# Seven half-block products for the up projections of a two-layer decoder step on one Trainium2 core

## The chip, the cores and the metric

The kernel runs on one core of one Trainium2 chip, as a single launch. A core has five engines with instruction queues of their own: PE (TensorE, matrix products into PSUM), DVE (VectorE), ACT (ScalarE), POOL (GpSimd) and SP (SyncE, which here only issues DMAs). Each works through its queue in order and waits on semaphores. The metric is the device time of one execution in microseconds (us). Before the change three runs took 1202.59, 1202.91 and 1203.35 us; the median, 1202.91, is the number to compare with.

## The reference

One inference step of a two-layer decoder trunk. 512 prompt rows and 8 x 4 sample rows, 544 in all, go through both layers: a token mixer (causal pooling in layer 0, a gated linear recurrence, HGRN2, in layer 1), then a gated feed-forward block with a causal convolution of width 3. The feed-forward block is what the change is about:

```python
D_MODEL, D_FF, CONV_W = 1024, 2816, 3

def conv_ffn(h, ctx, w_up, conv_w, conv_b, w_down):
    L = h.shape[1]
    u = h @ w_up                                  # (rows, 1024) @ (1024, 2 * 2816)
    full = jnp.concatenate([ctx.astype(u.dtype), u], axis=1)
    c = conv_b + sum(full[:, j:j + L] * conv_w[j] for j in range(CONV_W))
    gate, val = jnp.split(c, 2, axis=-1)
    y = (jax.nn.gelu(gate, approximate=True) * val) @ w_down
    return y, full[:, -(CONV_W - 1):]
```

Around every sub-layer stand RMS norms: `h = rmsnorm(x, norm_ffn_pre)`, and afterwards `x = x + rmsnorm(m, norm_ffn_post)`. All data are float32; the outputs are the rows after both layers and the new states.

## The kernel before

**Layout.** Features lie on the 128 partitions, the 544 rows (TOK) along the free axis, so x is 8 tiles (KT) of 128 x 544. A product is built from weight blocks of 128 output features; a block of an up projection has 8 k-tiles of 128 x 128.

**Precision.** Each float32 operand is split in two fp32r parts, high and low. `mm3` issues three matmuls for each k-tile and half of the rows: high by high, high by low, low by high. ACT makes the high part of a weight (`wh<-raw`), DVE the low part (`wl<-raw,wh`), 512 columns (four k-tiles) at a time. For some blocks (`DW`, `by_dma`) both parts come by DMA from POOL's queue instead: one plain load, a negated copy on ACT, one adding load.

**Feed-forward block** (`ffn`). The 2816 hidden features are 22 pairs of blocks (NPAIR), a gate block j and a value block 22 + j. PARTS = (8, 7, 7) cuts them into three parts. In each part all up blocks run first (`block`: 8 k-tiles x 2 halves x 3 matmuls, of 256 and 288 columns, into two PSUM banks of a tile `ps`); then the eight down products run over the pairs of that part, and DVE adds the second and third part to the sum `m`. The first six blocks go through `group`, which begins while the norm of the second half of the rows is still in work. After each up block:

- DVE multiplies the PSUM result by the row scale R of the norm (`evac_full`, into `t`),
- ACT and DVE make the convolution (`conv`: one ACT step, two DVE steps of 560 columns),
- after the value block, DVE multiplies it with the gelu of the gate, and ACT and DVE split the result for the down products (`finish`).

POOL copies the convolution's context in and out (`fst`) and, in the first part, issues the weight loads of `DW`.

**Order.** All of it is recorded by `Plan` and put in order at build time by a list scheduler (`emit`) with its own table of costs, latencies, and slots of the buffer pools; what comes out is a fixed order for each engine. Weights are one stream; `ensure(i + LOOK)` has the splits of the next three blocks recorded ahead. Raw weight tiles (`raw`, 128 x 1024) have 3 buffers, the split tiles (`wh`, `wl`) 10 each, the working tiles `t` 22, PSUM 2 double banks (`ps`) and 4 single ones (`pa`).

Of the kernel before, what the change touches and what calls it, by code (L numbers as in the profile page):

```python
# [36 lines left out]
PARTS = (8, 7, 7)  # L37
# [12 lines left out]
DW = ((2, 6), (3, 9), (3, 9))  # L50
# [289 lines left out]
def trunk_step(ctx: ExitStack, tc: _tile.TileContext, xT, xp, xs, spool, s0, fctx, par, gb0, cst, bands,  # L340
# [29 lines left out]
    up_i, dn_i = {}, {}  # L370

    def add_ffn(li):
        p0 = 0
        for pi, n in enumerate(PARTS):
            for j in range(p0, p0 + n):
                up_i[li, j] = len(stream)
                stream.append((wup[li, j], KT))
                up_i[li, NPAIR + j] = len(stream)
                stream.append((wup[li, NPAIR + j], KT))
            for o in range(KT):  # L380
                dn_i[li, pi, o] = len(stream)
                stream.append((wdn[pi][li, o], n))
            p0 += n
# [16 lines left out]
    bases = (0, min(hin_i.values()), min(up_i[1, j] for j in range(2 * NPAIR)))  # L400
# [5 lines left out]
    special = {}  # L406
    nxt = [0]

    def ensure(upto):
        while nxt[0] <= min(upto, len(stream) - 1):  # L410
            i = nxt[0]
            nxt[0] += 1
            src, kc = stream[i]
            if not by_dma(i):
                raw = tt((P, 512)) if kc * P <= 512 else wp.tile([P, KT * P], F32, tag="raw", name="raw")
                SP.dma_start(raw[:, 0:kc * P], src)
            chunks = []
            for c0 in range(0, kc, 4):
                n = min(4, kc - c0) * P
                if i in special:  # L420
                    sp, q = special[i]
                    wh, wl = sp[q + len(chunks)], sp[q + 2 + len(chunks)]
                else:
                    wh = wp.tile([P, 4 * P], F32R, tag="wh", name="wh", bufs=10)
                    wl = wp.tile([P, 4 * P], F32R, tag="wl", name="wl", bufs=10)
                if by_dma(i):

                    h, l, w = wh[:, 0:n], wl[:, 0:n], src[:, c0 * P:c0 * P + n]
                    POOL.dma_start(h, w)
                    ACT.activation(l, h.bitcast(F32), AF.Identity, scale=-1.0)  # L430
                    POOL.dma_start(l, w, accum_op=ALU.add)
                    chunks.append((wh, wl))
                    continue
                r = raw[:, c0 * P:c0 * P + n]
                ACT.activation(wh[:, 0:n], r, AF.Identity)
                DVE.tensor_tensor(wl[:, 0:n], r, wh[:, 0:n].bitcast(F32), op=ALU.subtract)
                chunks.append((wh, wl))
            prepared[i] = chunks
# [107 lines left out]
    x = one.tile([P, KT, TOK], F32, name="x")  # L546
# [117 lines left out]
    class Residual:  # L664
# [10 lines left out]
        def start_b(self, hf):  # L675
# [13 lines left out]
            def low(k):  # L689
                DVE.scalar_tensor_tensor(getx(ol)(k, sl), x[:, k, sl], pcol(gnext + k), oh[:, k, sl].bitcast(F32),  # L690
                                         op0=ALU.mult, op1=ALU.subtract)

# [133 lines left out]
    for hf, c in ((0, 0), (0, 4), (1, 0), (1, 4)):  # L826
        SP.dma_start(x[:, c:c + 4, HV[hf]], xT[:, c:c + 4, HV[hf]])
# [20 lines left out]
    def ffn(li, XH, XL, res, enter, mtile, leave, n_ahead, hv=HV):  # L848

        R = res.rnext  # L850
        cst_t = rp.tile([P, 17 * ROUND_A], F32, tag="fst", name="fst", bufs=1)[:, 0:2 * NPAIR * 18]
# [66 lines left out]
        def do_down(pi, o, src, sl):  # L918
            if o == 0 and pi == 2 and acc[0] is None:
                acc[0] = tt()  # L920
# [8 lines left out]
            if pi < 2:  # L929
# [10 lines left out]
        p0 = 0  # L940
        for pi, n in enumerate(PARTS):
            if pi == 1 and li == 0:
                plan.after(m0[:, KT - 1, :])
# [4 lines left out]
            j0 = p0  # L948
            blocks = []
            for j in range(p0, p0 + n):  # L950
                blocks += [j, NPAIR + j]
            if pi == 0:
                first, blocks = blocks[:GRP_U], blocks[GRP_U:]
                ensure(up_i[li, first[-1]])
                us_ = {}

                def each(g, o, hf):
                    if hf == 0:
                        us_[g] = new_u(first[g])
                    evac_half(*us_[g], o, hf)  # L960
                    if hf == 1:
                        finish(*us_[g], first[g])
                        ensure(up_i[li, first[g]] + GRP_U)
                group([up_i[li, j] for j in first], rH, rL, KT, each, enter(res), (4, 2),
                      (4, 2), (0, 1, 2, 3))
            for j in blocks:
                i = up_i[li, j]
                ensure(i + LOOK)
                t = block(i, rH, rL, KT, HP)
                u, us = new_u(j)  # L970
                evac_full(u, us, t)
                finish(u, us, j)
            yH = lambda k, sl: ys[j0 + k][0][:, sl]
            yL = lambda k, sl: ys[j0 + k][1][:, sl]

            i0, i1 = dn_i[li, pi, 0], dn_i[li, pi, 1]
            ensure(i1 + LOOK - 1)
            t0, t1 = ps2(), ps2()
            for ks in (range(n - 1), range(n - 1, n)):
                for t, i in ((t0, i0), (t1, i1)):  # L980
                    for k in ks:
                        for hf in range(2):
                            mm3(t[:, hf, 0:HT], i, k, yH, yL, slice(hf * HT, (hf + 1) * HT), k == 0, k == n - 1)
# [569 lines left out]
```

## Time and profile before

| | |
|---|---|
| median of three runs | 1202.91 us |
| the profiled execution | 1202.7 us, of which 1200.9 from first to last instruction |
| pooling mixer until the first up product of layer 0 | 0 to 42.8 us |
| feed-forward block, layer 0: up products of the three parts start at | 42.8, 196.1 and 322.1 us |
| its down products start at | 147.5, 279.8 and 405.8 us |
| HGRN2 mixer of layer 1 | 452.4 us, its output products from 726.9 us |
| down products of layer 1 start at | 878.6, 1011.9 and 1138.8 us |
| moved by DMA | 120.39 MB, 100 GB/s in the mean |

A row of the view of groups reads: line, engine, operation, written tile<-read tiles, shapes, count | busy us, mean ns of one | idle time before, and what ended it. L306 is the line of the scheduler that issues nearly everything, so groups are told apart by tile names: `wh`, `wl` weights, `raw` their float32 form, `ps` and `pa` PSUM, `t` working tiles, `xh`, `xl`, `oh`, `k` the split rows, `m` the sum of the down products. A row of the timeline reads: start us, length us, engine, the same names, count [idle before]. A row of a window reads: from:to, length, then busy us (x instructions) of PE, its weight loads, DVE, ACT and POOL, the granted clock of PE, and the DMA share.

### The profile page before, as it was taken

Reading aid. Unit: us, or ns where it says so; the run is one execution under the profiler, and the core shown is the slowest. Engines: PE = TensorE matmul, PEld = TensorE weight load, DVE = VectorE, ACT = ScalarE, POOL = GpSimd, SP = SyncE. Lnnn points to the kernel's source line nnn. Section 1 sums busy time; section 2 is a strip of 40 time slices with the busy share of each in tenths; the row PEclk is TensorE's granted clock in tenths of the full one; section 3 lists DMA queues with packets and bytes.
Section 4 is the critical chain, followed back from the end, with each engine's and each line's share of the span. In section 5 each row is a group of like instructions: output and inputs, shape, how many; then the busy total and the mean of one; then the engine's idle time right before and its main releaser. Section 6 shows DMA issues by size and latency. Waiting matters only on the chain.

```text
span 1200.9 us, 25513 instructions
## 1 busy us (share of the span) xinstructions
PE 1180.8 (98%) x10268; PEld 1147.4 (96%) x10268; DVE 777.6 (65%) x1809; ACT 561.2 (47%) x1139; POOL 215.7 (18%) x513
## 2 busy tenths in 40 slices
PE   8999999999999999999999999999999999999996
PEld 7899999999999997999999999999999999999995
DVE  6787733765367666688878985468742666457635
ACT  4655434443244455556555554546432444234441
POOL 3431101110011132111121131324100111011113
PEclk9999999999999999999999999999999999999998
DMA  9732222223222355423322223436222222322202
GB/s 320 169 91 71 89 88 88 88 78 99 88 89 97 106 142 127 107 87 104 109 94 83 90 91 120 124 63 149 86 82 86 84 83 75 106 88 84 78 30 75
DMA packets 43223, 120.39 MB, mean 100 GB/s; under 512 B 5339, under 2 KB 9819, under 8 KB 43097
## 3 DMA queue, kind: packets, MB, share of 16 engines
q1 hardware_dynamic: 30336, 91.71, 23.6%
q0 software_dynamic: 12624, 27.01, 9.5%
q8 instruction: 81, 1.33, 0.5%
q14 instruction: 38, 0.30, 0.1%
q10 hardware_dynamic: 144, 0.05, 0.0%
HBM read 110.79 MB, written 8.31 MB: 99 GB/s over the span
## 4 chain that ended last, share of the span: by engine, by line
PE 93%; DMA 3%; DVE 2%; ACT 1%; issue 0%; SPq 0%; DVEq 0%; ACTq 0%
PE ps L306 74%; PE pa L306 17%; PE pr L306 2%; DMA raw<-wup 1%; DMA k<-xp 1%; DVE t L306 1%; DVE m L306 1%; DMA k<-wup 0%; ACT t L306 0%; ACT wh L306 0%; PE pa L1449 0%; SPq L306 0%; DVE o L306 0%; ACT m L306 0%; DVE x L306 0%
## 5 line engine op out<-in xcount | busy, mean ns | idle before, releaser
L306 ACT ACTIVATE wh<-raw 128x512 fp32r<-128x512 f32 (+1 forms) x312 | 193.0, 620 | 336.9 <-PE ps L306 319.4
L306 PE MATMUL ps<-xh,wh 128*128 128x256 f32 (+1 forms) x1072 | 313.3, 292 | 0.0
L306 PE MATMUL ps<-xl,wh 128*128 128x256 f32 (+1 forms) x1072 | 309.8, 289 | 0.0
L306 PE MATMUL ps<-xh,wl 128*128 128x256 f32 (+1 forms) x1072 | 307.8, 287 | 0.0
L306 DVE TENSOR_TENSOR wl<-raw,wh 128x512 fp32r<-128x512 f32 (+1 forms) x312 | 210.0, 675 | 141.1 <-ACT wh L306 132.6
L306 PE MATMUL ps<-t,wh 128*128 128x272 f32 x1184 | 223.6, 288 | 0.8 <-ACT m L306 0.7
L306 PEld LDWEIGHTS ps<-xh,wl 128*128 128x128 f32 x1072 | 202.0, 188 | 2.8 <-issue 2.6
L306 PEld LDWEIGHTS ps<-xh,wh 128*128 128x128 f32 x1072 | 202.0, 188 | 2.5 <-issue 0.2
L306 PEld LDWEIGHTS ps<-xl,wh 128*128 128x128 f32 x1072 | 201.7, 188 | 2.6 <-issue 1.6
L306 PE MATMUL ps<-oh,wl 128*128 128x256 f32 (+2 forms) x688 | 198.4, 288 | 0.0
L306 PE MATMUL ps<-k,wh 128*128 128x256 f32 (+2 forms) x688 | 198.1, 288 | 0.0
L306 PE MATMUL ps<-oh,wh 128*128 128x256 f32 (+2 forms) x688 | 198.0, 288 | 0.0
L306 PEld LDWEIGHTS ps<-t,wh 128*128 128x128 f32 x1184 | 185.6, 188 | 1.7 <-ACT m L306 1.1
L306 DVE TENSOR_TENSOR t<-t 128x512 f32<-128x512 f32 (+10 forms) x332 | 141.3, 450 | 52.1 <-ACT t L306 46.4
L306 PE MATMUL ps<-t,wl 128*128 128x272 f32 x592 | 170.4, 288 | 0.0
L306 DVE SCALAR_TENSOR_TENSOR t<-t,prm 128x560 f32<-128x560 f32 (+1 forms) x184 | 146.8, 801 | 36.1 <-ACT t L306 33.1
L306 POOL COPY fst<-t 128x16 f32<-128x16 f32 (+1 forms) x176 | 73.0, 450 | 439.8 <-DVE t L306 439.5
L306 DVE TENSOR_TENSOR t<-ps,R 128x512 f32<-128x512 f32 (+1 forms) x216 | 86.3, 433 | 76.0 <-PE ps L306 74.4
L306 ACT ACTIVATE t<-t 128x544 fp32r<-128x544 f32 (+5 forms) x145 | 85.5, 600 | 98.8 <-DVE t L306 95.7
L306 PEld LDWEIGHTS ps<-k,wh 128*128 128x128 f32 x688 | 129.7, 189 | 0.5 <-issue 0.5
L306 PEld LDWEIGHTS ps<-oh,wh 128*128 128x128 f32 x688 | 129.8, 189 | 0.0
L306 PEld LDWEIGHTS ps<-oh,wl 128*128 128x128 f32 x688 | 129.2, 188 | 0.0
(174 smaller groups left out, 1645.3 us busy)
## 6 DMA issues: line engine op xcount, KB each, us to landing
raw<-wup SPq DMA_DIRECT2D x78, 512.0 KB, 3.3
raw<-wdn SPq DMA_DIRECT2D x32, 448.0 KB, 3.3
raw<-win SPq DMA_DIRECT2D x26, 512.0 KB, 3.3
raw<-wdn SPq DMA_DIRECT2D x16, 512.0 KB, 3.2
wh<-wup POOLq DMA_DIRECT2D x16, 256.0 KB, 3.6
wl<-wup POOLq DMA_DIRECT2D x16, 256.0 KB, 5.7
t<-s POOLq DMA_DIRECT2D x16, 256.0 KB, 4.0
o_hs<-t POOLq DMA_DIRECT2D x16, 256.0 KB, 2.4
```

The costliest lines, as they stand in the source:

```text
L306: o[1](*o[3], **o[4])
```

## The change

The pairs 6 to 21 of each layer (16 of 22) are computed with seven products of half blocks. A and B are the two weight blocks of a pair, each cut in two along k (512 columns each); the rows are cut in two halves of 272 (U). For each pair:

- **Weights.** `seventh` forms seven 512-column operands: four are halves of A and B as loaded, three are sums, made by four additions on POOL. All seven are split in high and low on ACT and DVE, in place of four splits before. Both raw tiles stay until the last split.
- **Rows.** `operands`, once a layer during part 0, forms the sums and differences of the row halves from x, its gain and R (so R no longer comes in afterwards); DVE scales, POOL adds, ACT and DVE split (`both`). They take the place of x and of the tiles xh and xl; x is therefore saved to yT and loaded again after the last such pair.
- **Products.** `seven` runs 7 x 4 x 3 matmuls of 272 columns into three `pa` banks, some started and some added to, with a step on ACT or DVE after each product to combine them.

Down products now have five parts, PARTS = (6, 4, 4, 3, 5); those of a part are spread between the pairs of the next one by MIX; weights are recorded nine units of four k-tiles ahead. DVE adds four parts to `m` instead of two. More blocks have their weights made by DMA: entries 2 to 11 instead of 2 to 5 of layer 0, 3 to 11 instead of 3 to 8 of layer 1.

```diff
-PARTS = (8, 7, 7)
+PARTS = (6, 4, 4, 3, 5)
+MIX = ((4, 4, 0, 0), (3, 3, 2, 0), (3, 3, 2), (2, 2, 2, 2, 0))
+SEVEN = PARTS[0]
-DW = ((2, 6), (3, 9), (3, 9))
+DW = ((2, 12), (3, 9), (3, 12))
...
+    def seventh(i, q):
+        H = 4 * P
+        if q == 0:
+            raws[i] = A_, B_ = [wp.tile([P, KT * P], F32, tag="raw", name="raw") for _ in range(2)]
+            for t, src in zip((A_, B_), stream[i][0]):
+                SP.dma_start(t, src)
+            mine[i] = dict(sums) or {q: tt((P, H)) for q in range(2)}
+            POOL.tensor_tensor(mine[i][0], A_[:, 0:H], B_[:, 0:H], op=ALU.add)
+            POOL.tensor_tensor(B_[:, 0:H], B_[:, 0:H], B_[:, H:2 * H], op=ALU.add)
+            POOL.tensor_tensor(mine[i][1], B_[:, 0:H], A_[:, 0:H], op=ALU.add)
+        A_, B_ = raws[i]
+        if q == 6:
+            POOL.tensor_tensor(A_[:, H:2 * H], A_[:, H:2 * H], mine[i][1], op=ALU.add)
+        return (mine[i][1], A_[:, 0:H], mine[i][0], B_[:, 0:H], A_[:, H:2 * H], B_[:, H:2 * H], A_[:, H:2 * H])[q]
...
+        def operands(k, out):
+            za, hold = tt(), out["hold"]
+            zb, w, s_ = hold[:, k], hold[:, 6 + k % 2], hold[:, 4 + k // 2, U[k % 2]]
+            for z, f in ((za, k), (zb, k + 4)):
+                DVE.scalar_tensor_tensor(z, x_of(f), pcol(gn + f), R, op0=ALU.mult, op1=ALU.mult)
+                SP.dma_start(yT[:, f], x_of(f))
+            POOL.tensor_tensor(w[:, U[0]], za[:, U[1]], zb[:, U[1]], op=ALU.subtract)
+            POOL.tensor_tensor(w[:, U[1]], za[:, U[0]], za[:, U[1]], op=ALU.subtract)
+            POOL.tensor_tensor(za[:, U[1]], za[:, U[0]], w[:, U[0]], op=ALU.subtract)
+            POOL.tensor_tensor(s_, zb[:, U[0]], za[:, U[1]], op=ALU.subtract)
+            both(out["a", k], za)
...
+            Y, X, Z = banks
+            c, t = w[:, U[0]], w[:, U[1]]
+            after = (lambda: ACT.activation(c, Y, AF.Identity),
+                     lambda: DVE.tensor_tensor(t, c, X, op=ALU.subtract),
+                     lambda: DVE.tensor_tensor(c, t, Z, op=ALU.add),
+                     lambda: second(1, ALU.subtract, c, Y),
+                     lambda: ACT.activation(u_of(0)[0][:, 2:2 + HT], X, AF.Identity),
+                     lambda: DVE.tensor_tensor(u_of(1)[0][:, 2:2 + HT], c, Z, op=ALU.add),
+                     lambda: second(0, ALU.subtract, Y, t))
+            for q, (o, more) in enumerate(((Y, 0), (X, 0), (Z, 0), (Y, 0), (X, 1), (Z, 0), (Y, 1))):
+                ahead_units(unit0[i] + q)
+                wh, wl = prepared[i][q]
+                for k in range(4):
+                    xh_, xl_ = operand(q, k)
+                    sl = slice(k * P, (k + 1) * P)
+                    for e, (a, b) in enumerate(((wh, xh_), (wh, xl_), (wl, xh_))):
+                        PE.matmul(o, a[:, sl], b, start=(not more and k == 0 and e == 0), stop=(k == 3 and e == 2),
+                                  skip_group_check=True)
+                after[q]()
...
+        sums.clear()
+        for q in range(4):
+            xt[q] = big.tile([P, 2, TOK], F32, tag=f"X{q}", name="x")
+            SP.dma_start(xt[q], yT[:, 2 * q:2 * q + 2])
```

How this moves instructions is seen in the order on three engines. First DVE, near the end of the first part of layer 0 before the change: one pair of blocks (evacuations from `ps_374` and `ps_382`), with the weight splits of later blocks (`wl`) in between.

```order
L306 TENSOR_TENSOR t_375<-ps_374,R0_106 128x512
L306 TENSOR_TENSOR t_375<-ps_374,R0_106 128x8x4
L306 TENSOR_TENSOR wl_392<-raw_388,wh_391 128x512
L306 SCALAR_TENSOR_TENSOR t_376<-t_375,prm_79,t_376 128x560 x2
L306 TENSOR_TENSOR wl_398<-raw_396,wh_397 128x512
L306 TENSOR_TENSOR t_383<-ps_382,R0_106 128x512
L306 TENSOR_TENSOR t_383<-ps_382,R0_106 128x8x4
L306 TENSOR_TENSOR wl_400<-raw_396,wh_399 128x512
L306 SCALAR_TENSOR_TENSOR t_384<-t_383,prm_79,t_384 128x560 x2
L306 TENSOR_TENSOR wl_409<-raw_407,wh_408 128x512
```

And DVE in part 2 of layer 0 after it: pair 10 is combined from its three banks (`pa_550`, `pa_551`, `pa_552` are Y, X and Z), with splits of pair 11 in between (`raw_559` and `raw_560` are its two blocks, `sums` and `fst` hold POOL's sums).

```order
L312 TENSOR_TENSOR t_553<-t_553,pa_551 128x272
L312 TENSOR_TENSOR wl_562<-raw_559,wh_561 128x512
L312 TENSOR_TENSOR t_553<-t_553,pa_552 128x272
L312 TENSOR_TENSOR wl_564<-sums_389,wh_563 128x512
L312 TENSOR_TENSOR t_565<-t_553,pa_550 128x240
L312 TENSOR_TENSOR t_565<-t_553,pa_550 128x8x4
L312 TENSOR_TENSOR wl_567<-raw_560,wh_566 128x512
L312 TENSOR_TENSOR wl_570<-raw_559,wh_569 128x512
L312 TENSOR_TENSOR t_565<-t_553,pa_552 128x272
L312 TENSOR_TENSOR wl_572<-raw_560,wh_571 128x512
L312 TENSOR_TENSOR t_568<-pa_550,t_553 128x240
L312 TENSOR_TENSOR t_568<-pa_550,t_553 128x8x4
```

Each result of a pair is now put together in several short steps, and seven splits a pair stand between them instead of four.

POOL in the same stage: before the change it only copies contexts in (`t<-fst`) and out (`fst<-t`).

```order
L306 COPY fst_228<-t_394 128x2
L306 COPY fst_228<-t_394 128x16
L306 COPY fst_228<-t_402 128x2
L306 COPY fst_228<-t_402 128x16
L306 COPY t_480<-fst_228 128x8x2
L306 MEMSET t_480 128x2
```

After it, three weight sums of pair 8 (`raw_467`, `raw_468`) stand in a row, and the fourth after two copies.

```order
L312 TENSOR_TENSOR sums_389<-raw_467,raw_468 128x512
L312 TENSOR_TENSOR raw_468<-raw_468 128x512
L312 TENSOR_TENSOR fst_230<-raw_468,raw_467 128x512
L312 COPY fst_230<-t_462 128x16
L312 COPY fst_230<-t_462 128x2
L312 TENSOR_TENSOR raw_467<-raw_467,fst_230 128x512
```

So POOL has 128 additions of 512 columns that it did not have, and they read and write the tiles that ACT and DVE split.

On SP after the change, the raw tiles of the pairs 8 to 11 are loaded one after another, two for each pair, from a pool of three.

```order
L312 DMA raw_467<-wup 128x1024
L312 DMA raw_468<-wup 128x1024
L312 DMA raw_491<-wup 128x1024
L312 DMA raw_492<-wup 128x1024
L312 DMA raw_514<-wup 128x1024
L312 DMA raw_515<-wup 128x1024
L312 DMA raw_559<-wup 128x1024
L312 DMA raw_560<-wup 128x1024
```

Before, a raw tile belonged to one block and was free after two splits; now a pair holds two of the three until its last splits.

More of the change, by code (lines that the diff above doesn't have):

```diff
@@ L398, in trunk_step @@
     add_ffn(1)
[L400 removed]
+    bases = (0, min(hin_i.values()), up_i[1, 0])
     def by_dma(i):
@@ L412, in ensure @@
             nxt[0] += 1
             src, kc = stream[i]
[L414 to L437, printed above, removed]
@@ L545, in trunk_step, with xs_of, x_of @@
     load_tok(3)
-    x = one.tile([P, KT, TOK], F32, name="x")
+    xt = [big.tile([P, 2, TOK], F32, tag=f"X{q}", name="x") for q in range(4)]
+    def xs_of(k0, k1, sl):
+        return xt[k0 // 2][:, k0 % 2:k0 % 2 + k1 - k0, sl]
+    def x_of(k, sl=slice(0, TOK)):
+        return xt[k // 2][:, k % 2, sl]
     ident = cs[:, C_ID:C_ID + P]
@@ new lines, in ffn @@
+        up(GRP_U // 2)
+        out, late = homes()
+        out["hold"] = big.tile([P, KT, TOK], F32, tag=mtag, name="hold")
+        for j in range(GRP_U // 2 + 1, PARTS[0]):
+            for k in range(2):
+                operands(2 * (j - GRP_U // 2 - 1) + k, out)
+            up(j)
+        late(out)
+        for k in range(4):
+            both(out["z", k], out["hold"][:, k])
+        for k in range(2):
+            both(out["s", k], out["hold"][:, 4 + k])
+        rest = rp.tile([P, TOK], F32, tag="R", name="sums")
@@ L942, in ffn @@
+        sums.update({0: rest[:, 0:4 * P], 1: fst[:, 2 * NPAIR * 18:2 * NPAIR * 18 + 4 * P]})
+        mtile = big.tile([P, KT, TOK], F32, tag=mtag, name="m")
+        for pi in range(1, len(PARTS)):
+            for kind, q in mixed(pi):
+                if kind == "down":
+                    down(pi - 1, q)
+                else:
+                    up(q)
             if pi == 1 and li == 0:
-                plan.after(m0[:, KT - 1, :])
+                plan.after(mtile[:, KT - 1, :])
                 lower_bounds()
@@ L947, in ffn @@
                 POOL.memset(Asp, 0.0)
[L948 to L983, printed above, removed]
@@ L1014, in trunk_step, with homes1 @@
+    def homes1():
+        h, l = (big.tile([P, 4, TOK], F32R, tag=f"P1{q}", name="op") for q in range(2))
+        return home(lambda k: (h[:, k], l[:, k]), lambda k: ol[k], lambda k: ol[4 + k], "P2")
     lbm = one.tile([P, 8, KT], F32, name="lbm")
```

258 lines of the change are left out of this document (196 added, 62 removed).

## The prediction, made before the changed kernel ran

> **What bounds the kernel now.** I read the page first: busy times, slices, chain.
>
> ```profile
> span 1200.9 us, 25513 instructions
> PE 1180.8 (98%) x10268; PEld 1147.4 (96%) x10268; DVE 777.6 (65%) x1809; ACT 561.2 (47%) x1139; POOL 215.7 (18%) x513
> PE   8999999999999999999999999999999999999996
> PEclk9999999999999999999999999999999999999998
> PE 93%; DMA 3%; DVE 2%; ACT 1%; issue 0%; SPq 0%; DVEq 0%; ACTq 0%
> ```
>
> PE is busy in nearly every slice, at its full granted clock, and 93% of the chain that ended last is PE. A busy PE proves little by itself, so I take its pace from the chain in order of time (start, length, instructions):
>
> ```profile
> 87.91 70.90 PE ps L306 x569
> 160.03 129.67 PE ps L306 x1038
> 290.50 125.92 PE ps L306 x1008
> ```
>
> 70.90/569, 129.67/1038 and 125.92/1008 are all 0.125 us a matmul, with about 1 us between the pieces. So in the FFN the kernel lasts as long as its matmuls are many. Next, how full the other engines are there: up projections (1st, 3rd and 5th stretch) and down products (2nd and 4th), in layer 0.
>
> ```profile
> core 0: us, PE busy (x) PEld busy (x) DVE busy (x) ACT busy (x) POOL busy (x), PEclk, DMA share, GB/s
> 100.00:147.00 47.00, 47.00 (x380) 47.00 (x379) 34.35 (x60) 22.09 (x32) 6.65 (x18) 1.00 0.27 91
> 148.00:196.00 48.00, 47.65 (x381) 47.43 (x380) 14.52 (x23) 14.67 (x25) 4.57 (x32) 1.00 0.27 88
> 197.00:279.00 82.00, 82.00 (x661) 82.00 (x660) 57.48 (x108) 39.63 (x57) 10.16 (x28) 1.00 0.27 85
> 280.00:322.00 42.00, 41.94 (x335) 41.72 (x334) 18.56 (x30) 11.04 (x18) 3.31 (x24) 1.00 0.30 99
> ```
>
> DVE is 70 to 73% busy under up projections and 30 to 44% under down products; the load is uneven. The change moves work to DVE and POOL, so the question is whether PE stays the bound.
>
> **What PE saves.** A pair of blocks took 2 x 8 x 2 x 3 = 96 matmuls; seven products of 4 k-tiles take 7 x 4 x 3 = 84, of 272 columns, the mean of the 256 and 288 of before. Down products keep their number (22 k-tiles x 8 x 6 a layer). So 12 x 16 pairs x 2 layers = 384 matmuls go: 384 x 0.125 = **48.0 us**. The profiled execution took 1202.7 us (span 1200.9, and 1.8 around it), 0.2 under the median of 1202.91. If nothing else came to matter: 1202.7 - 48.0 = 1154.7 us.
>
> **What DVE gets.** Its pace is read from starts in its timeline (start, length, count); lengths overlap by some 0.08.
>
> ```profile
> 240.25 1.64 DVE L306 SCALAR_TENSOR_TENSOR t<-t,prm 128x560 f32<-128x560 f32 x2 [0.41 <-ACT t L306]
> 241.81 0.68 DVE L306 TENSOR_TENSOR wl<-raw,wh 128x512 fp32r<-128x512 f32 x1
> ...
> 247.65 0.69 DVE L306 TENSOR_TENSOR wl<-raw,wh 128x512 fp32r<-128x512 f32 x1
> 248.26 0.79 DVE L306 TENSOR_TENSOR t<-t 128x512 f32<-128x512 f32 x2
> 249.77 0.72 DVE L306 TENSOR_TENSOR t<-t 128x544 fp32r<-128x544 f32 x1 [0.73 <-ACT t L306]
> 250.41 0.78 DVE L306 TENSOR_TENSOR t<-ps,R 128x512 f32<-128x512 f32 x2
> 251.11 0.68 DVE L306 TENSOR_TENSOR wl<-raw,wh 128x512 fp32r<-128x512 f32 x1
> ```
>
> A 512-wide weight split takes 248.26 - 247.65 = 0.61, two convolution steps 241.81 - 240.25 = 1.56, 544 elements 0.64, 512 + 32 elements 0.70. By the same slope (1.1 ns an element) 272 take about 0.35 and 240 + 32 about 0.41; these two are estimates. A seven-product pair then costs DVE 7 x 0.61 (splits) + 2 x 1.56 (convolution) + 0.70 + 0.64 (gate by value, low part) + 3 x 0.35 + 2 x 0.41 (recombining from PSUM) = 10.6 us. Cross-check: today's pair takes 57.48 x 12/82 = 8.4; less 4 splits and 2 evacuations (2.4 + 1.4), plus 4.3 and 1.9, it is 10.8. Down products, 8 a part: 6 wide 0.61 + 0.33, 4 wide 0.61 + 0.64 (twice, now with an addition from PSUM each), 3 wide 0.47 + 0.64: 7.5 + 10 + 10 + 8.9 = 36.4. In the stage with the 16 pairs and these four parts DVE has 16 x 10.6 + 36.4 = **206 us** per layer. PE has 16 x 10.5 + 17 k-tiles x 8 x 6 x 0.125 = 168 + 102 = **270 us**. DVE alone fits.
>
> **What POOL gets.** Four 512-wide weight sums a pair, a new thing for it. The nearest rows are its sums of 544 and 256 elements, and its copies:
>
> ```profile
> L306 POOL TENSOR_TENSOR t<-t 128x544 f32<-128x544 f32 x9 | 12.3, 1363 | 68.4 <-ACT t L306 68.4
> L306 POOL TENSOR_TENSOR x<-x,m 128x256 f32<-128x256 f32 x4 | 3.0, 791 | 4.1 <-DVE m L306 4.1
> L306 POOL COPY fst<-t x176: 184/542/1294, 72.4 to 1140.3; 128x2 f32<-128x2 f32 x88, 128x16 f32<-128x16 f32 x88
> ```
>
> (The last row: least, median and longest ns.) A 512-wide sum lies between 0.79 and 1.36; scaled from 1.363, the nearer row, it is 1.28 us, which I take. 4 x 1.28 + 6 copies of at least 0.18 = 6.2 a pair, 99 us a layer (68 to 105 by the two ends): it fits by itself too. But the two engines do not run freely side by side. At the kernel's end POOL adds 288-wide rows while DVE works (POOL's row first, then DVE's, then DVE's mean for the same form):
>
> ```profile
> 1180.33 4.20 POOL L306 TENSOR_TENSOR x<-x,m 128x288 f32<-128x288 f32 x4
> 1181.24 1.71 DVE L306 TENSOR_TENSOR m<-m,t 128x288 f32<-128x288 f32 x2
> 1182.87 1.01 DVE L306 TENSOR_TENSOR t<-t 128x256 f32<-128x256 f32 x1
> 1183.80 0.41 DVE L306 TENSOR_TENSOR m<-m,pa 128x256 f32<-128x256 f32 x1
> L306 DVE TENSOR_TENSOR t<-t 128x256 f32<-128x256 f32 x92 | 37.5, 428 | 11.6 <-ACT t L306 9.9 <-POOL t L306 1.3 <-PE pa L306 0.2
> ```
>
> With both inputs in SBUF, a 256-wide sum takes 1.01 instead of 0.43, the two 288-wide ones 1.71; the one that reads PSUM (pa) takes its usual 0.41 within the same run of POOL sums. So I treat POOL's sums and DVE's two-SBUF-input work as one queue. The Trainium skill says the same under "SBUF — State Buffer", section "Who interferes with whom": a Vector instruction with two SBUF inputs and a GpSimd instruction that reads SBUF exclude each other for a whole instruction; these rows agree, and by that rule weight sums on POOL are not free, which speaks against this change.
>
> The price, between two bounds. Upper: nothing overlaps, 206 + 99 = 305, 35 above PE's 270. Lower: all PSUM-reading DVE work (16 x 1.9 + 24 x 0.64 = 45 us) lies beside POOL; 206 - 45 + 99 = 260, under 270, cost nothing. I take the middle that the mix gives: 45/206 = 22% of DVE's work lets POOL pass, so 22 of its 99 us are hidden, 283 in all, **13 us a layer**, 26 in two. This reaches PE in two ways: a bank is rewritten three products (4.5 us from its own start, 3 us from its end) later, so late recombining stops PE; and weight splits run only some ten half-blocks ahead. It is worst where pairs follow each other with few down products between: part 4 (pairs 17 to 21) has 5 x 10.5 + 8 x 2.25 = 70.5 us of PE against 5 x (10.6 + 6.2) + 8.9 = 93 of DVE and POOL.
>
> **The rest.** ACT: 39.63 x 12/82 = 5.8 a pair now; three more splits and two copies of 272 (0.63 and at most 0.63 each by the first row below) make at most 9 of 10.5; with the down work (about 27 a layer) 171 of 270. Hidden.
>
> ```profile
> L306 ACT ACTIVATE wh<-raw 128x512 fp32r<-128x512 f32 x280 | 176.1, 631 | 305.8 <-PE ps L306 288.9 <-DMA raw<-wup 5.8 <-PE pa L306 4.6
> L306 POOL DMA_DIRECT2D wl<-wup x16 | 15.2, 1120 | 3.9 <-ACT wl L306 3.3 <-issue 0.4
> L306 POOL DMA_DIRECT2D wh<-wup x16 | 8.9, 561 | 18.9 <-DVE c L306 9.6 <-PE pa L306 6.7 <-PE pr L306 2.2
> raw<-wup SPq DMA_DIRECT2D x78, 512.0 KB, 3.3
> ```
>
> Part 0 (six ordinary pairs, 72 us) also builds operands: 8 scalings (0.78 at most) and 14 low parts (0.64), 15 us of DVE, and 16 half-width sums, 11 of POOL. DVE there is 34.35 of 47, so 53 of 72; weights made by DMA take 12 splits off it in layer 0 and 6 in layer 1 (7.3 and 3.7). 53 + 15 - 5 + 11 is 74 against 72: cost 0 to 4 a layer; I take 0, since some of it reads PSUM. The 18 more weight halves by DMA cost POOL 18 x (1.12 + 0.56) = 30 us over both layers while it is mostly idle; behind them on POOL stand the operand sums, and PE would wait for these only at the first seven-product pair, which starts with operands ready early and has down products put between. On SP, 16 saves of x and its 8 reloads join loads at a DMA share of 0.3; the reload is needed only 30 us later, after the last down products. Were that cover gone, it would cost one landing, some 3 us a layer.
>
> **Rivals.**
>
> *All hidden*: POOL's sums fall into DVE's gaps and PSUM work (the 260 above). For: PE idles today in no slice of the FFN. Against: the order was fixed without regard to that one queue. Time 1155 to 1163.
>
> *The raw buffers become the loop.* Each seven-product pair needs two of three raw tiles, so its second tile loads only after the last split of the pair before. Then 3.3 (landing) + 3 x 1.28 + 0.63 + 0.69 to the first split, 4 x 0.61 to the fifth, 1.28 + 0.63 + 0.69 to the last: 13.4 us, about 16 with hand-overs. PE takes 10.5 a pair where no down products stand between (8 to 10, 13 to 14, 21) and 15 in part 4. Uncovered this costs 3 x 2.9 = 9 to 3 x 5.5 + 4 x 1 = 20 a layer; half of it lies where the shared queue costs anyway, so about 7 on top: 1180.7 + 14 = 1195.
>
> *Slower: the shared queue takes it all.* If POOL passes hardly any DVE work (hidden share under a tenth), the stage costs the full 35 or, with in-order waits, more. The break-even is 24 a layer: 305 - h - 270 = 24, h = 11 of POOL's 99 us. With h = 0 it is 1154.7 + 70 = 1225. For: DVE's order is fixed, so whatever waits behind a blocked split waits too. Against: the rows at 1183.80.
>
> *It does not do what it says*: the order shows 84 matmuls a pair; I give this no chance.
>
> **How the numbers follow.** Forecast: 1154.7 + 26 = **1180.7**, own range 1164 to 1192, chance 0.45. All hidden 0.18; raw loop 0.15; shared queue saturated 0.22, from about 1200 to 1225. About 0.2% (2.4 us) is what a measurement of this kernel tells from no change. Of the raw loop and the saturated queue 0.02 each fall within it. Faster 0.45 + 0.18 + 0.13 = 0.76, same 0.04, slower 0.20. Range 1155 to 1211: all of the forecast and the raw loop, nearly all of the first rival, and under half of the last.
>
> **What would show it.** Right: some 384 fewer matmuls at 0.125; in FFN stretches DVE near 80% busy or more and POOL near 40%, DVE's splits lengthened from 0.69 mean towards 1; PE gaps released by DVE, most between pairs 17 and 21. If PE's gaps are ended by DMA raw or by POOL sums with DVE idle, it is the raw loop. If DVE's splits keep 0.69 beside POOL sums, the shared queue is wrong; if PE's pace per matmul changes, the 48 us are.

## The result and the profile after

The changed kernel takes **1218.8 us** (median of 4 runs, 1218.57 to 1220.61), the kernel before beside it on the same chip 1203.13 (4 runs, 1202.59 to 1205.02). The ratio is 1.0131, with a 95% interval of 1.0113 to 1.0148: about 16 us slower, where the prediction had said 22 us faster. The profiled execution took 1218.57 us, 1216.7 of it span.

First the page of the changed kernel: span, busy times, PE's slices, the granted clock, the chain that ended last.

```profile
span 1216.7 us, 25725 instructions
PE 1157.7 (95%) x9892; PEld 1116.1 (92%) x9892; DVE 963.7 (79%) x2075; ACT 632.7 (52%) x1343; POOL 475.1 (39%) x709
PE   8999898999999999999999999999899999999895
PEclk9999999999999999999999999999899999999998
PE 58%; DVE 23%; issue 7%; ACT 6%; POOL 4%; DMA 2%; DVEq 0%; SPq 0%; ACTq 0%; POOLq 0%
```

PE issues 376 matmuls fewer by the records (384 by the code), so the saving is there. But PE's share of the chain fell from 93% to 58%, and DVE has 23% of it. "PE 95% busy" hides this: a matmul that waits for its clock or stands in short gaps still fills the slice. The windows of 25 us (and one of 290) say more; the number behind x is what counts.

```profile
150.00:175.00 25.00, 25.00 (x201) 25.00 (x200) 20.06 (x36) 16.36 (x31) 7.69 (x8) 1.00 0.34 112
200.00:225.00 25.00, 21.27 (x144) 20.62 (x143) 20.42 (x34) 13.33 (x23) 10.79 (x16) 0.86 0.23 75
275.00:300.00 25.00, 22.10 (x159) 21.41 (x158) 22.56 (x38) 12.18 (x23) 11.42 (x24) 0.93 0.20 64
350.00:375.00 25.00, 21.80 (x159) 21.35 (x159) 21.62 (x40) 12.01 (x23) 10.21 (x14) 0.93 0.18 59
140.00:430.00 290.00, 275.46 (x2099) 271.59 (x2098) 237.42 (x403) 141.29 (x254) 126.12 (x182) 0.97 0.29 95
```

An undisturbed window has 201 matmuls, 25/201 = 0.124 us each: the pace did not change. Others have 144 to 159, a fifth to over a quarter fewer. In the whole stage of seven-product pairs of layer 0 (140 to 430 us) there are 2099 where 290 x 201/25 = 2332 would fit. DVE is 82% busy there (237.42/290), POOL 43%: neither is full in the mean.

Next, the groups of DVE's two commonest forms with two SBUF inputs, before the change and after it (mean ns behind the comma), and POOL's weight sums after it:

```profile
L306 DVE TENSOR_TENSOR wl<-raw,wh 128x512 fp32r<-128x512 f32 x280 | 192.4, 689 | 135.2 <-ACT wh L306 126.7 <-PE pa L306 5.1
L306 DVE SCALAR_TENSOR_TENSOR t<-t,prm 128x560 f32<-128x560 f32 x176 | 140.6, 802 | 35.0 <-ACT t L306 32.3
```

```profile
L312 DVE TENSOR_TENSOR wl<-raw,wh 128x512 fp32r<-128x512 f32 x262 | 188.1, 729 | 56.2 <-ACT wh L312 50.0 <-PE pa L312 5.1
L312 DVE SCALAR_TENSOR_TENSOR t<-t,prm 128x560 f32<-128x560 f32 x176 | 185.0, 1084 | 21.3 <-ACT t L312 20.8
L312 POOL TENSOR_TENSOR sums<-raw 128x512 f32<-128x512 f32 x30 | 40.5, 1349 | 39.4 <-DMA raw<-wup 34.4 <-ACT t L312 4.9
L312 POOL TENSOR_TENSOR raw<-raw 128x512 f32<-128x512 f32 x32 | 49.7, 1552 | 2.4
```

The convolution step of the same shape went from 802 to 1084 ns, the weight split only from 689 to 729. POOL's first sum of a pair takes 1349 ns, the second, which stands directly behind it, 1552. Both sides are stretched. The means hide how much, since most instructions of a group have no sum beside them. Counted in the trace, the 75 convolution steps that stand beside a sum on POOL take 1474 ns in the mean and the other 101 take 795; of the 262 weight splits only 26 stand beside a sum, and they take 1135 ns against 684; the 272-wide steps that read PSUM (`t<-t,pa`) take 434 beside a sum and 429 without.

One such place in the timeline, 361 to 370 us (start, length), engine by engine: POOL, DVE, ACT, PE.

```profile
361.08 1.29 POOL L312 TENSOR_TENSOR sums<-raw 128x512 f32<-128x512 f32 x1 [0.30 <-DMA raw<-wup]
362.45 1.67 POOL L312 TENSOR_TENSOR raw<-raw 128x512 f32<-128x512 f32 x1
364.20 1.67 POOL L312 TENSOR_TENSOR fst<-raw 128x512 f32<-128x512 f32 x1
...
361.48 1.50 DVE L312 SCALAR_TENSOR_TENSOR t<-t,prm 128x560 f32<-128x560 f32 x1 [0.99 <-ACT t L312]
363.52 2.95 DVE L312 SCALAR_TENSOR_TENSOR t<-t,prm 128x560 f32<-128x560 f32 x2
367.02 0.79 DVE L312 SCALAR_TENSOR_TENSOR t<-t,prm 128x560 f32<-128x560 f32 x1
...
366.50 0.67 ACT L312 ACTIVATE t<-t 128x560 f32<-128x560 f32 x1 [4.32 <-DVE t L312]
368.95 0.61 ACT L312 ACTIVATE wh<-sums 128x512 fp32r<-128x512 f32 x1
369.47 0.37 ACT L312 ACTIVATE t<-pa 128x272 f32<-128x272 f32 x1
...
369.89 0.51 PE L312 MATMUL pa<-op,wh 128*128 128x272 f32 x2 [2.20 <-ACT t L312]
```

Of four equal convolution steps, the three that stand beside POOL's sums take 1.50 and 2 x 1.48 us, the last, after them, 0.79: some 2.1 us lost. ACT idles 4.32 us until the third is done (its own next step is the gelu), then works off the gelu, two splits for a down product and three splits of weights (three rows between are left out), and only then comes the copy of bank Y out of PSUM at 369.47, for which PE has waited 2.20 us. (Of a pair's seven operands four are POOL sums and three are halves as loaded; the description of the change has it the other way round.) So PE's gap is put down to ACT, which is 52% busy in the mean, and the delay comes from DVE's steps beside POOL's sums, two engines further back. In the whole run PE waited 12 times, 16.0 us, for such copies (`PE pa <- ACT t` in the waits).

What follows the gap is a second loss (windows behind it):

```profile
369.90:374.30 4.40, 4.40 (x23) 4.40 (x24) 4.33 (x10) 1.65 (x3) 1.53 (x3) 0.62 0.00 0
374.30:378.70 4.40, 4.40 (x37) 4.40 (x37) 2.87 (x6) 1.89 (x4) 1.73 (x3) 1.00 0.31 95
```

The granted clock falls to 0.62 in the mean of 4.4 us (0.50 from 371.0 to 374.2): 23 matmuls, "4.40 us busy", instead of the 37 of the next 4.4 us, or 14 x 0.12 = 1.7 us more. There are nine such slow stretches between 40 and 1187 us; the kernel before has none there (both kernels have some at the start or the end). The mean clock is 0.981 instead of 0.994; 1.3% of 1217 us is some 16 us, an upper estimate of this loss, since an idle PE loses nothing by a slow clock.

### The profile page after: what moved, and what is told of

It is laid out like the page before. It is cut to its first block, busy times and chain, and to the rows that moved or that the text cites. A ratio compares the mean times of both kernels' runs of the same rounds, so it can differ in the third digit from the quotient of the medians.

```text
span 1216.7 us, 25725 instructions
## 1 busy us (share of the span) xinstructions
PE 1157.7 (95%) x9892; PEld 1116.1 (92%) x9892; DVE 963.7 (79%) x2075; ACT 632.7 (52%) x1343; POOL 475.1 (39%) x709
## 3 DMA queue, kind: packets, MB, share of 16 engines
q8 instruction: 78, 1.28, 0.4%
## 4 chain that ended last, share of the span: by engine, by line
PE 58%; DVE 23%; issue 7%; ACT 6%; POOL 4%; DMA 2%; DVEq 0%; SPq 0%; ACTq 0%; POOLq 0%
PE ps L312 30%; PE pa L312 27%; DVE t L312 13%; DVE wl L312 5%; ACT t L312 3%; DVE m L312 2%; ACT wh L312 2%; PE pr L312 2%; POOL raw L312 1%; POOL fst L312 1%; DMA t<-bands 1%; DVE k L312 1%; DVE op L312 1%; POOL wh L312 0%; DMA k<-wup 0%
## 5 line engine op out<-in xcount | busy, mean ns | idle before, releaser
L312 PE MATMUL pa<-op,wh 128*128 128x272 f32 x1152 | 268.8, 298 | 23.6 <-ACT t L312 15.6
L312 ACT ACTIVATE wh<-raw 128x512 fp32r<-128x512 f32 (+2 forms) x294 | 172.7, 597 | 168.6 <-PE ps L312 68.0
L312 DVE TENSOR_TENSOR wl<-raw,wh 128x512 fp32r<-128x512 f32 (+2 forms) x294 | 199.5, 691 | 59.4 <-ACT wh L312 53.1
L312 PEld LDWEIGHTS pa<-op,wh 128*128 128x128 f32 x1152 | 200.3, 195 | 29.5 <-ACT t L312 18.9
L312 PE MATMUL pa<-op,wl 128*128 128x272 f32 x768 | 226.3, 295 | 0.9 <-DVE wl L312 0.9
L312 PE MATMUL ps<-xh,wh 128*128 128x256 f32 (+1 forms) x560 | 166.4, 298 | 0.0
L312 PE MATMUL ps<-xl,wh 128*128 128x256 f32 (+1 forms) x560 | 162.3, 290 | 0.5 <-DVE xl L312 0.5
L312 PE MATMUL ps<-xh,wl 128*128 128x256 f32 (+1 forms) x560 | 160.9, 288 | 0.4 <-DMA wl<-wup 0.4
L312 PEld LDWEIGHTS pa<-op,wl 128*128 128x128 f32 x768 | 149.6, 195 | 1.1 <-DVE wl L312 1.1
L312 PE MATMUL pa<-k,wh 128*128 128x272 f32 (+2 forms) x560 | 139.5, 293 | 4.6 <-ACT k L312 3.4
```

The costliest lines, as they stand in the source:

```text
L312: o[1](*o[3], **o[4])
```

## The experiments

Each ratio is to the kernel before on the same chip. In the first expectations theories have letters: A is the clash of POOL's and DVE's reads of SBUF, B the loop of raw tile, sums and splits being too long, C that DVE's own longer work is too much; D (from the fifth on) is that the uneven spread of the down products costs time, E that an even spread alone changes nothing.

**1. The four weight sums on DVE.**

```diff
-            POOL.tensor_tensor(mine[i][0], A_[:, 0:H], B_[:, 0:H], op=ALU.add)
+            DVE.tensor_tensor(mine[i][0], A_[:, 0:H], B_[:, 0:H], op=ALU.add)
...
```

> The four weight sums of each seven-product pair are made on DVE instead of POOL. Theory A (POOL's sums and DVE's two-SBUF-input work shut each other out, so DVE is late, ACT behind it, PE waits and its clock halves): DVE gets 4 x 0.61 x 16 = 39 us more a layer, 206 + 39 = 245 of 270 us, and POOL's sums are gone from the shared queue; PE's gaps shrink to a third, 1165 to 1190 us. Theory B (the loop raw tile, three sums, splits, next raw tile is too long): only the sums get shorter, 1200 to 1215. Theory C (DVE simply has too much work): more of it, over 1222.

1207.39 us (1205.01 to 1209.08), ratio 1.003 [1.002, 1.004]: 11 us better, although DVE has 128 instructions more. A's range, 1165 to 1190, is missed; the time lies in B's, and C's is excluded. Taking the sums off POOL is worth more than DVE's extra load costs, but that load isn't free, so this run alone does not tell A from B.

**2. No sums.** The four additions are left out; the splits read the halves as loaded.

```diff
-            POOL.tensor_tensor(mine[i][0], A_[:, 0:H], B_[:, 0:H], op=ALU.add)
...
-        return (mine[i][1], A_[:, 0:H], mine[i][0], B_[:, 0:H], A_[:, H:2 * H], B_[:, H:2 * H], A_[:, H:2 * H])[q]
+        return (A_[:, 0:H], A_[:, 0:H], A_[:, H:2 * H], B_[:, 0:H], A_[:, H:2 * H], B_[:, H:2 * H], A_[:, H:2 * H])[q]
```

> The four weight sums are left out; halves of the two blocks stand in for them (the products are not those of the scheme). It gives the whole price of the sums, wherever it arises. Theory A: 1160 to 1178, DVE splits back at 0.69 mean. Theory B: 1175 to 1195, since the raw tiles still come round three by three. Theory C: 1205 to 1218, DVE's own work is unchanged.

1180.97 us (1177.7 to 1183.57), ratio 0.9821 [0.9802, 0.9839]. The weight sums cost 1218.8 - 1181.0 = **37.8 us**. The time is 3 us above A's range and inside B's, so this run does not separate the two either. Two windows of this kernel, at places where the changed kernel had 144 and 159 matmuls, and the whole stage:

```profile
200.00:225.00 25.00, 21.00 (x158) 20.78 (x157) 16.61 (x33) 12.45 (x21) 2.47 (x6) 0.93 0.23 75
350.00:375.00 25.00, 25.00 (x202) 25.00 (x201) 22.41 (x44) 14.39 (x27) 2.91 (x6) 1.00 0.21 66
...
140.00:430.00 290.00, 286.00 (x2269) 285.67 (x2270) 226.10 (x432) 161.31 (x283) 42.31 (x127) 0.99 0.33 109
```

The second is full again, so its loss was the sums'. The first is not: there pairs without down products follow each other, and PE waits 4.00 us for ACT's copy of a bank at 206.13 us. ACT's queue ahead of that copy holds a wait for DVE and a table load of 1.28 us.

**3. POOL as busy, but not reading.** In place of each sum two POOL memsets write the same columns; the scheduler gets a price for them.

```diff
-            POOL.tensor_tensor(mine[i][0], A_[:, 0:H], B_[:, 0:H], op=ALU.add)
+            POOL.memset(mine[i][0], 0.5)
+            POOL.memset(mine[i][0], 0.25)
...
```

> Each weight sum on POOL is replaced by two memsets of the same 512 columns (the sums are left out): POOL is busy for about as long (two of about 0.51 us for one of about 1.28) and stands at the same place in the chain from raw tile to split, but reads nothing. Theory A: no clash left, within 8 us of the kernel without sums, 1163 to 1185, though POOL stays busy. Theory B: the chain is nearly as long as with sums, 1205 to 1217. Theory C: 1210 to 1219.

1183.68 us (1180.47 to 1186.86), ratio 0.9836 [0.9814, 0.9857]. From the page and the groups of this kernel:

```profile
PE 1144.5 (97%) x9892; PEld 1110.5 (94%) x9892; DVE 911.1 (77%) x2075; ACT 641.3 (54%) x1343; POOL 405.3 (34%) x837
L314 DVE SCALAR_TENSOR_TENSOR t<-t,prm 128x560 f32<-128x560 f32 x176 | 143.0, 840 | 22.2 <-ACT t L314 21.6
L314 POOL MEMSET raw<- 128x512 f32 x128 | 67.7, 529 | 76.4 <-DMA raw<-wup 33.4 <-DVE wl L314 32.3 <-ACT t L314 6.0
```

The time lies in A's range (1163 to 1185) and 21 us under B's. POOL is busy for 405.3 us against 276.0 without sums, with the same writes in the same places and the same raw buffers held for them, and it costs 2.7 us, about the spread of the runs. DVE's step is at 840 ns (835 in 2). So some 35 of the 37.8 us are POOL's *reads*, against DVE's. A pair of memsets takes 1.06 us, somewhat less than a sum (1.35 to 1.55), so a small part could still be POOL's time as such.

**4. The spread alone**, with all 22 pairs as ordinary blocks, without operands and without the reload of x.

```diff
-SEVEN = PARTS[0]
+SEVEN = NPAIR
...
...
```

> Only the other half of the change: five parts, down products spread between the pairs, weights ahead by units, the new DMA entries; all 22 pairs in ordinary products, no operands, no weight sums. All three theories: PE has as many matmuls as before, so 1200 to 1206, the same as before within 0.3%. Over 1210 would say that the spreading itself costs, and that part of the 64 us lost is due to it.

1198.28 us (1197.09 to 1199.47), ratio 0.9957 [0.9942, 0.9972]. That is 2 us under the range expected: five parts, spread down products and the new DMA entries gain about 5 us by themselves. With 48.0 us of matmuls off that, the floor for seven products in this frame is 1198.3 - 48.0 = 1150.3 us, a sum and not a run.

**5. An even spread**: two down products behind each of the 16 pairs.

```diff
-PARTS = (6, 4, 4, 3, 5)
+PARTS = (6, 4, 4, 4, 4)
-MIX = ((4, 4, 0, 0), (3, 3, 2, 0), (3, 3, 2), (2, 2, 2, 2, 0))
+MIX = ((2, 2, 2, 2),) * 4
```

> The changed kernel with its down products spread evenly: parts of 6, 4, 4, 4 and 4 pairs, two down products behind every seven-product pair (no pairs in a row without any). POOL keeps the sums. Theory D (the gaps at pairs 8 to 10 and 17 to 21 come from the uneven spread: DVE and POOL need more than PE's 10.5 us where no down product stands between): the same work, but every period now has 16.5 to 19.5 us of PE against 10.6 + 6.2 + 2.5 = 19.3 of DVE and POOL, so only a part comes back: 1198 to 1212. Rival E (the spread does not matter, the clash of sums alone sets the time): 1215 to 1222.

1216.86 us (1213.28 to 1221.27), ratio 1.0117 [1.0087, 1.0146]: E's range has it; by the medians an even spread gains 2 us while POOL adds. It makes the loss readable, though. PE's gaps in this kernel's timeline, and the windows of the stage and of one period:

```profile
252.71 0.52 PE L312 MATMUL pa<-op,wh 128*128 128x272 f32 x2 [0.68 <-ACT t L312]
254.69 0.40 PE L312 MATMUL pa<-op,wh 128*128 128x272 f32 x1 [0.20 <-DVE t L312]
270.69 0.52 PE L312 MATMUL pa<-op,wh 128*128 128x272 f32 x2 [0.65 <-ACT t L312]
272.67 0.39 PE L312 MATMUL pa<-op,wh 128*128 128x272 f32 x1 [0.20 <-DVE t L312]
...
140.00:430.00 290.00, 277.35 (x2167) 272.90 (x2166) 253.06 (x414) 147.76 (x257) 118.24 (x178) 1.00 0.32 109
252.71:270.69 17.98, 17.12 (x132) 16.68 (x132) 16.52 (x26) 8.82 (x16) 7.42 (x8) 1.00 0.25 88
```

The same gaps come back after 270.69 - 252.71 = 17.98 us, where PE needs 10.5 + 2 x 3.0 = 16.5 for a pair and two down products four wide. Something other than PE has a period of 18.0 us; DVE is busy for 16.52 of them. The granted clock is full here, so this loss needs no slow clock.

**6. Even spread and the sums on DVE** (the edits of 1 and 5).

> The even spread, and the four weight sums on DVE. A period has 16.5 us of PE against 10.6 + 2.4 + 2.5 = 15.5 of DVE, and POOL reads little. Theory D: DVE fits in every period, so the 207 and 283 us gaps of the kernel with sums on DVE go; left are the two hand-overs at the first seven-product pair of each layer (some 8 us each with the halved clock): 1178 to 1195. Rival C (DVE has too much work whatever the spread): 1202 to 1210.

1193.15 us (1190.74 to 1199.66), ratio 0.9931 [0.9907, 0.9955]: 14 us better than 1, 24 better than 5, and in D's range (1178 to 1195). With the sums on DVE the even spread is worth 14 us, with the sums on POOL only 2; why so little there was not settled.

**7. Even spread, three sums by adding DMAs** from POOL's queue, the fourth on DVE. The scheduler counts 1.5 us more for such a DMA.

```diff
...
-            POOL.tensor_tensor(mine[i][0], A_[:, 0:H], B_[:, 0:H], op=ALU.add)
-            POOL.tensor_tensor(B_[:, 0:H], B_[:, 0:H], B_[:, H:2 * H], op=ALU.add)
-            POOL.tensor_tensor(mine[i][1], B_[:, 0:H], A_[:, 0:H], op=ALU.add)
+            POOL.dma_start(s1, src_a[:, 0:H])
+            POOL.dma_start(s0, src_a[:, 0:H])
+            POOL.dma_start(s1, src_b[:, 0:H], accum_op=ALU.add)
+            POOL.dma_start(s0, src_b[:, 0:H], accum_op=ALU.add)
+            POOL.dma_start(s1, src_b[:, H:2 * H], accum_op=ALU.add)
+            POOL.dma_start(B_[:, 0:H], src_b[:, H:2 * H], accum_op=ALU.add)
...
-            POOL.tensor_tensor(A_[:, H:2 * H], A_[:, H:2 * H], mine[i][1], op=ALU.add)
+            DVE.tensor_tensor(A_[:, H:2 * H], A_[:, H:2 * H], mine[i][1], op=ALU.add)
```

> The even spread, and three of the four weight sums made by adding DMAs from POOL's queue (six DMAs a pair), the fourth on DVE. DVE 10.6 + 0.6 + 2.5 = 13.7 of 16.5 us, and no sums on POOL. Theory A with D: 1165 to 1185. Rival B (the chain from load to split is what counts; it is now three DMAs of some 5 us each in a row): PE waits for weights at each pair, over 1195.

1189.51 us (1186.41 to 1198.15), ratio **0.9899 [0.9865, 0.9933]**: faster than both kernels, with the widest scatter of all. It lies between A's range with D (1165 to 1185) and B's (over 1195).

**8. As 7, with the last parts 3 and 5 wide again** (PARTS of the change, MIX one to three behind every pair).

> The kernel of e7 (even spread, three sums by adding DMAs, the fourth on DVE), with the last parts again 3 and 5 wide instead of 4 and 4; the down products stay evenly spread. Theory: e7's PE gaps at the exits of the feed-forward blocks (4.2 us and 3.9 us in e6, where the last part is also 4 wide) come from DVE being late with the last pair, and a longer last part covers them: 3 to 8 us under e7, so 1182 to 1187 us. Rival: the gaps at the exits only move to the start of the last down products, and the time stays at 1189 to 1192.

1193.58 us (1190.42 to 1196.51), ratio 0.9919 [0.9906, 0.9931]. The theory, 1182 to 1187, was wrong. In the profiled executions PE's wait at the end of layer 0's block is 1.05 us instead of 3.17, but one of 6.59 us stands at 366 us, where 7 has none.

**9 and 10. The operand sums of part 0 on DVE**, in kernel 8 and in the changed kernel.

```diff
-            POOL.tensor_tensor(w[:, U[0]], za[:, U[1]], zb[:, U[1]], op=ALU.subtract)
+            DVE.tensor_tensor(w[:, U[0]], za[:, U[1]], zb[:, U[1]], op=ALU.subtract)
...
```

> As e8, with the four half-width sums of the row operands (4 times a layer, in part 0) on DVE instead of POOL, so that no POOL sum is left beside DVE there. Theory: the PE gap ahead of the first seven-product pair (about 4 to 6 us a layer, with a window at the halved clock behind it) is the same clash as in the weight sums; without it the gap goes down by at least half, 3 to 6 us a layer, 6 to 12 us under e8. Rival: the gap is the length of the chain from the last product of part 0 to the first operand, or DVE's own load there; then the time stays within 3 us of e8 or goes up.

> The changed kernel with only the operand sums moved from POOL to DVE; its weight sums stay on POOL. By the theory of the clash the gaps ahead of the first seven-product pair (3.5 us in layer 0, 3.8 + 1.3 us in layer 1) shrink and the time falls by 4 to 10 us from 1218.8, to 1209 to 1215. By the rival (length of the chain, or DVE's load) it stays between 1216 and 1222.

In kernel 8 nothing: 1192.01 us (1186.12 to 1194.59), 0.9903 [0.9884, 0.9923]. In the changed kernel 1210.25 us (1207.02 to 1211.53), ratio 1.0053 [1.004, 1.0067], **8.5 us** better. There the gap in front of the first seven-product pair is gone in layer 0, and in layer 1 PE's longest wait there falls from 3.67 to 1.25 us. The changed kernel's timeline (POOL, DVE, PE), then that of kernel 10 (DVE):

```profile
125.14 2.46 POOL L312 TENSOR_TENSOR t<-t,hold 128x272 f32<-128x272 f32 x2
127.56 2.47 POOL L312 TENSOR_TENSOR hold<-hold,t 128x272 f32<-128x272 f32 x2
...
127.11 1.07 DVE L312 TENSOR_TENSOR k<-t,k 128x544 fp32r<-128x544 f32 x1
128.10 1.29 DVE L312 TENSOR_TENSOR xl<-hold,op 128x544 fp32r<-128x544 f32 x1
...
127.14 0.64 PE L312 MATMUL pa<-k,wh 128*128 128x272 f32 x3 [3.37 <-ACT k L312]
```

```profile
124.78 0.43 DVE L312 TENSOR_TENSOR hold<-t 128x272 f32<-128x272 f32 x1
128.03 0.72 DVE L312 TENSOR_TENSOR k<-t,k 128x544 fp32r<-128x544 f32 x1
```

A half-width sum takes 1.23 us on POOL and 0.43 on DVE, and beside POOL's sums the 544-wide low parts (0.72 alone) take 1.07 to 1.29. In kernel 9 the gap at this place went as well (in layer 1 from 4.87 us to 0.26), but others of up to 4.33 us stand at other places than in 8, and the sum stayed the same: the rival's range.

**11. No POOL sums at all**: weight sums left out as in 2, operand sums on DVE, spread of 8.

> The changed kernel with no POOL sums at all: the four weight sums of a pair are left out (as in e2), the operand sums are on DVE (as in e10), and the down products are spread evenly between the pairs (PARTS as in the change). By the theory that POOL's sums were the whole loss, now also those of the operands, it comes to within 10 us of the floor of 1150 us (1198.3 of e4 less 48.0): e2's 1181.0 less the 8.5 us that e10 gained and less the uneven spread, 1158 to 1170. Rival: DVE's own load in seven-product pairs (10.6 us beside 10.5 of PE) stops PE even without a clash; then it stays at 1171 to 1181.

1166.2 us (1165.04 to 1168.24), ratio 0.9693 [0.9676, 0.971]. The window of the seven-product stage, and the two hand-overs to it:

```profile
140.00:430.00 290.00, 289.32 (x2302) 289.06 (x2301) 229.30 (x444) 162.81 (x286) 39.54 (x130) 1.00 0.35 115
...
100.00:140.00 40.00, 37.39 (x292) 36.48 (x291) 38.81 (x75) 23.74 (x41) 7.60 (x17) 1.00 0.23 59
840.00:860.00 20.00, 15.57 (x105) 14.71 (x106) 18.08 (x35) 10.87 (x20) 2.67 (x4) 0.91 0.14 47
```

With DVE 79% busy (229.30/290), PE runs 2302 matmuls in the 290 us, 99% of what fits: C falls, and the time is in the range expected (1158 to 1170). DVE's own work in the pairs stops nothing; it is too much only around the operands, where DVE is busy 38.81 of 40 us and 30 and 56 matmuls are missing, about (30 + 56) x 0.124 = 11 of the 15.9 us that still lie above the floor of 1150.3.

**12. All four sums by adding DMAs**, otherwise as 9.

```diff
-            DVE.tensor_tensor(A_[:, H:2 * H], A_[:, H:2 * H], mine[i][1], op=ALU.add)
+            POOL.dma_start(A_[:, H:2 * H], mine[i][1], accum_op=ALU.add)
```

> As e9 (even spread, three sums by adding DMAs, operand sums on DVE), with the fourth sum made by an adding DMA as well, so that neither POOL nor DVE adds weights. If what separates e9 (1192.0) from the kernel without sums (e11, 1166.2) is DVE's 32 additions (0.61 us each, 20 us), the time falls by 5 to 15 us, to 1177 to 1187. If it is the landing of the adding DMAs, which the last split of each pair then waits for as well, it stays at 1189 to 1197 or rises.

1223.35 us (1220.61 to 1229.88), ratio 1.0184 [1.0158, 1.0211], 31 us worse than 9. From the DMA issues and ACT's waits of this kernel (us, times, longest):

```profile
raw<-wup SPq DMA_DIRECT2D x69, 512.0 KB, 5.4
raw<-sums POOLq DMA_DIRECT2D x16, 256.0 KB, 5.7
raw<-fst POOLq DMA_DIRECT2D x14, 256.0 KB, 6.5
...
ACT wh L312 <- DMA raw<-fst: 40.5, 11, 8.9
ACT wh L312 <- DMA raw<-sums: 31.9, 11, 6.5
```

The last sum can start only when the split of the same columns is done, and its landing of 5.7 to 6.5 us is then on the path of the pair's last split. With the adding loads, plain weight loads land in 5.4 us instead of 3.3. That also bears on 7 to 9, where they land in 4.5 to 4.7: these gave up the clash for DMA traffic and 0.61 us of DVE a pair, and 7 and 8 keep the operand sums on POOL. What makes up their 23 to 27 us over 11 was not settled.

## Why the prediction was wrong

**PE's 48.0 us: right.** 9892 matmuls instead of 10268, at 0.124 us as before.

**DVE's and POOL's work: right.** In kernel 11 DVE has 229.30 us in 290, 213 in 270, where 206 were costed, and PE isn't stopped. A POOL sum was taken as 1.28 us; it is 1.35 first in line, 1.55 in the clash.

**One queue for POOL's sums and DVE's two-SBUF-input work: right.** Kernel 3 shows it: busy but not reading, POOL cost 2.7 us, reading 37.8. The rule quoted from the Trainium skill, "SBUF — State Buffer", section "Who interferes with whom", fits: the memsets write only, and DVE's convolution step stayed at 840 ns beside them, against 1084 in the kernel with sums; that page exempts GpSimd instructions that only write. Of the signs named, DVE's and POOL's shares came as forecast (82% and 43% in the stage). The splits' mean did not move towards 1 us (0.73), since only 26 of 262 meet a sum; those take 1.14. And PE's gaps are mostly ended by ACT, not by DVE.

**The price of that queue, "13 us a layer, 26 in two": this step failed.** The weight sums cost 37.8 us (kernel 2). The step added up DVE and POOL over the stage of 16 pairs, hid 22% of POOL's time, and set the sum, 283, against PE's 270. So PE's surplus at pairs with many down products paid for the pairs without any, though PE is only about three products (some 3 us) and ten half-blocks of weights ahead of DVE and POOL. Added up pair by pair, with MIX as it is and nothing carried over, the same figures lose more: 15.4 - 10.5 = 4.9 us at each of the four pairs without down products, 2.6 at the four pairs of part 4 with two, and 1.4 at the two pairs with two products four wide. That is 19.6 + 10.4 + 2.8 = 33 a layer. In the 290 us of layer 0 the changed kernel is 233 matmuls short of 2332, some 29 us; kernel 2, without the sums, is 63 short, some 8 us. For kernel 5 the sum by pairs gives 12 x 1.4 = 17 a layer, and its 165 missing matmuls are some 20 us. For its period the sum gives 10.6 + 2 x 1.25 + 0.78 x 6.2 = 17.9 us and the trace 17.98, closer than the inputs allow, as POOL's sums took 1.35 to 1.55 us and not 1.28.

So the traces lie nearer to the sum by pairs than to the mean. A mean with nothing hidden, the 35 a layer of the upper bound, would fit the 29 too, but not the 20 of kernel 5. That averaging was the error is argued from these windows, not shown: by the sum by pairs kernel 5 should be some 32 us faster than the changed kernel, and it is 2 by the medians (9 in the 290 us of layer 0). The prediction had named the bunching itself ("worst where pairs follow each other"; 93 us against 70.5 in part 4), and then used the mean.

**Part 0, "cost 0 to 4 a layer; I take 0": this step failed too.** Moving the operand sums off POOL gains 8.5 us in two layers (kernel 10), and with them on DVE the hand-over still costs some 11 in two (kernel 11). The sum had come to 74 us of work for 72 of PE, but it was spread over the whole part in thought; the operands come last in it, and the first seven-product pair waits for them.

**ACT "hidden": right in load, wrong in order.** At 52% busy it stands in most of PE's waits, because its queue holds steps that wait for DVE, and splits that wait for POOL's sums (38.0 us in 18 waits for `raw`), ahead of copies that PE waits for.

**Not priced: the clock.** A slow stretch of 3.4 us costs up to 1.7 us at half clock, and one of 6.8 us up to 3.4. The predicted 1180.7 had no term for it. In the differences measured above it is included.

**The rivals.** "The shared queue takes it all" (1200 to 1225) had the sign and the time: the range given, 1155 to 1211, took in only its lower part and missed 1218.8. Its condition, that POOL passes hardly any DVE work, does not hold for the steps that read PSUM (434 ns beside a sum, 429 without), and nearly half of the loss lies outside the sums: 1218.8 is 1150.3 (floor with the spread's own 5 us) + 15.9 (kernel 11) + 14.8 (kernel 2 over 11: operand sums, uneven spread) + 37.8. Of the miss of 38.1 us, 11.8 are the sums' price (37.8 instead of 26) and 30.7 what had been taken as nothing, less 4.4 that the floor lies under 1154.7. These are differences between kernels and add up by construction; taken in another order they could be cut otherwise, as the operand sums show (8.5 us in the changed kernel, 1.6 between 8 and 9). The raw-buffer loop is small: in kernel 3 memsets stand in that loop in place of the sums, and it is 2.7 us over 2; in kernel 11 a pair still takes two of the three raw tiles, and PE does 99% of what fits. That most gaps would lie between pairs 17 and 21 was wrong too: the window at 200 us, where pairs 8 and 9 have no down products, loses more than any other of the stage.

## What to carry to other kernels

The load of two engines that shut each other out is better summed over the stretch that the buffers between them and the bounding engine can bridge, here about a pair, than over a stage: a surplus of PE elsewhere may pay for nothing. Work at a hand-over is set against the time it has there, not against a whole part. Before giving idle POOL a sum of SBUF tiles, ask what DVE pays for it: here 0.61 us of DVE's own time was cheaper than 1.35 us of POOL's, since the sums on POOL cost 37.8 us and those on DVE 26.4 (1207.4 - 1181.0). And saved matmuls are worth their time only if no gap opens, as a gap can cost twice, once as a wait and once at the slower clock behind it.

## What the runs showed of the hardware

The granted clock of PE fell to half after rather short gaps, and their length alone does not decide it. In the changed kernel the first of these two gaps was followed by 3.4 us at half clock, the second, as long, by none:

```profile
294.53 0.64 PE L312 MATMUL ps<-t,wh 128*128 128x272 f32 x3 [1.98 <-ACT t L312]
...
1126.67 0.52 PE L312 MATMUL pa<-op,wh 128*128 128x272 f32 x2 [1.94 <-ACT t L312]
```

All nine stretches last 3.4 or 6.8 us. Matmuls are recorded as busy all through them; only their count gives them away.

A DVE step with two inputs in SBUF took nearly twice its time beside a sum on POOL (1474 against 795 ns), a step that reads PSUM its usual time (434 against 429), and beside memsets, which read nothing, the mean of the first hardly moved (840 against 835).
